# Modulation chunks in two output products and a new schedule for VectorE's share, in a two-block transformer on one core

## The chip, the cores and the metric

One NeuronCore of a Trainium2 chip runs the whole program in one launch. The metric is the device time of one execution in microseconds (us); smaller is better.

## The reference

Two blocks of two layers each work on 256 tokens of width 1024, with 256 context tokens beside them in the first layer of each block. All arithmetic is fp32. What the change touches is the modulation: every layer multiplies the activation of a condition vector with a 1024 x 6144 matrix, once for the tokens and once for the context, and cuts the result into six parts (shift, scale and gate of the mixer, shift, scale and gate of the FFN).

```python
# block 1, one layer
m_lat = [m[:, None, :] for m in jnp.split(jax.nn.silu(c) @ ada_w[l] + ada_b[l], 6, axis=-1)]
h_lat = modulate(x_lat, m_lat[0], m_lat[1])            # x * (1 + scale) + shift
y_lat, y_ctx = even_mixer(...) if l % 2 == 0 else odd_mixer(...)   # both end in y @ w_out
x_lat = layer_norm(DN_ALPHA * x_lat + m_lat[2] * y_lat, ln_g[l, 0], ln_b[l, 0])
f_lat = conv_ffn(modulate(x_lat, m_lat[3], m_lat[4]), ...)          # up, conv of 3, silu(g)*a, down
x_lat = layer_norm(DN_ALPHA * x_lat + m_lat[5] * f_lat, ln_g[l, 1], ln_b[l, 1])
# block 2, one layer: rms_norm in place of layer_norm, a mixer of three gated branches, SwiGLU
h = rms_norm_2(xl, g_pre_mix[l]) * (1.0 + sc1) + sh1
y, yc = token_mixer(h, hc, ...)                                     # ends in m @ w_out
xl = xl + gt1 * rms_norm_2(y, g_post_mix[l])
h = rms_norm_2(xl, g_pre_ffn[l]) * (1.0 + sc2) + sh2
xl = xl + gt2 * rms_norm_2(swiglu(h, w_ffn_in[l], w_ffn_out[l]), g_post_ffn[l])
```

In the first layer of a block the context runs through the same steps (512 tokens in all, "T=512"); in the second only the 256 tokens do ("T=256").

## The kernel before

A product of an fp32 weight is made of three TensorE products: SyncE (SP) loads a weight tile of 512 KB (`wr`, 4 buffers), ScalarE casts it (`wh`, L162), VectorE subtracts (`wl`, L164; 3 buffers of each), and TensorE multiplies the high parts and the two mixed pairs (`mm3`; the data's halves are `hH`/`hL`, `gH`/`gL`, `yH`/`yL`). SP issues its loads in program order, and a load waits until its `wr` buffer is free.

The program runs in stages: `even_mixer` (to about 266 us of the span), `b1_out` (the mixer's output product, residual and layer norm, then 128x128 transposes, L370, of the normalised rows `z`), `b1_ffn` with T=512, `odd_mixer`, `b1_out` (T=256), `b1_ffn` (T=256), then block 2: `b2_mixer` and `b2_ffn` with T=512, `b2_mixer` (2070 to 2437 us) and `b2_ffn` with T=256. The even mixer's order is written by a planner that weaves the projection's products with the attention's steps; elsewhere a scheduler orders each engine's instructions by the program's order and its own estimate of when they are ready.

A modulation part (`ada`, `a0` to `a3` for the four layers) is a list of items: eight chunks of 128 x 1024 weights, then a bias and, for most parts, a turn (two transposes, L243). A chunk has two forms. As *quarters* (L198 on `wr`) TensorE multiplies it with the condition at once. On VectorE (`onto`, L205 and L208) each of one or two condition rows is one `adacc` instruction, and at the part's end TensorE sums the result with *pick* products (L198 on `adacc`). A chunk is a load in the `wr` buffers in either form.

Who places the items: the even mixer takes them with `stream_ada` (so many items to each of its six groups, the rest at its end); the T=512 FFNs take them on VectorE with `share_ada`, which adds a number (`SHARE`) to a credit at each call, after an up pair (`up_share`) and after every unit of a down product (`each`), and issues the chunks that the credit pays for; the T=256 FFN of block 1 takes one chunk per up pair (`run_ada`). In a T=512 FFN the order is: up pairs j = 0 to 10, the down product of their outputs in two halves (`nb`) of six units, the evacuation of each half (`tm`, L1098, and `x`, L1101), up pairs 11 to 21, and the second down product. `idle_work` holds the layer norm's affine steps, put off into the up pairs.

## Time and profile before

| | |
|---|---|
| median of 3 runs | 2647.53 us (2646.34 to 2651.3) |
| the profiled execution | 2645.67 us, span 2643.9 us |
| TensorE busy | 2506.0 us (95%) |
| VectorE busy | 1914.5 us (72%) |
| ScalarE busy | 1226.1 us (46%) |
| mean granted TensorE clock | 0.982 |
| loads on SP's queue | 386.45 MB, 47.0% of the 16 DMA engines' span |
| chain that ended last | TensorE 68%, VectorE 15%, issue 5%, ScalarE 5%, DMA 4% |

Busy shares are means over stages with different limits. The granted clock is a share of 2.4 GHz; a stretch at 0.5 runs at 1.2 GHz.

### The profile page before, as it was taken

What the parts mean: (1) busy time and instruction counts of PE and PEld (TensorE: products, weight loads), DVE (VectorE), ACT (ScalarE), POOL (GpSimd) and SP (SyncE); (2) the same over time, 40 slices, a digit from 0 to 9 for tenths busy, and PEclk for the clock granted to TensorE, in tenths of its full rate; (3) what the DMA queues carried; (4) which work ended last, traced back from release to release, by engine and by line L of the source; (5) the groups of instructions that cost most, each with busy time, mean ns of one, the idle gap of its engine ahead of it and who ended that gap; (6) DMA issues with size and microseconds to landing.
All of it is one profiled execution on the core that took longest, in us unless ns stands there. A gap on an engine that the chain in (4) does not pass through costs nothing.

```text
span 2643.9 us, 40529 instructions
## 1 busy us (share of the span) xinstructions
PE 2506.0 (95%) x15364; PEld 2181.9 (83%) x15364; DVE 1914.5 (72%) x3347; ACT 1226.1 (46%) x2329; POOL 323.2 (12%) x411
## 2 busy tenths in 40 slices
PE   7998999899998899999989999999999999898998
PEld 5887797688876898899877878887887999798997
DVE  5866887776878977557779855767666788886554
ACT  3655463134455555556652233632224556554543
POOL 5321100000131000242320000001000100000000
PEclk9999999999999899999989999999999999999999
DMA  8344664664656676531212334556774522356564
GB/s 272 102 127 153 225 184 132 192 205 138 189 172 209 206 234 199 172 91 54 61 50 88 88 100 147 176 177 210 245 234 144 156 80 62 102 155 211 170 181 147
DMA packets 129827, 412.36 MB, mean 156 GB/s; under 512 B 16640, under 2 KB 24992, under 8 KB 129632
## 3 DMA queue, kind: packets, MB, share of 16 engines
q1 hardware_dynamic: 119296, 386.45, 47.0%
q0 software_dynamic: 10048, 23.30, 2.8%
q8 instruction: 121, 1.98, 0.3%
q14 instruction: 74, 0.61, 0.1%
q10 hardware_dynamic: 288, 0.02, 0.0%
HBM read 408.59 MB, written 1.11 MB: 155 GB/s over the span
## 4 chain that ended last, share of the span: by engine, by line
PE 68%; DVE 15%; issue 5%; ACT 5%; DMA 4%; POOL 2%; SPq 0%; DVEq 0%; POOLq 0%; ACTq 0%
PE mm L171 62%; DVE wl L164 3%; PE ax L171 3%; POOL rs_r L310 1%; DMA wr<-in_ada_w 1%; ACT wh L162 1%; DMA s0w<-in_ada_w 1%; PE ax L629 1%; PE ax L618 1%; DVE ptl L633 1%; DVE adacc L208 1%; PE mm L198 1%; DMA wr<-in_w_mod 1%; ACT p L1526 1%; DVE cv L1669 1%
## 5 line engine op out<-in xcount | busy, mean ns | idle before, releaser
L162 ACT CAST wh<-wr 128x1024 fp32r<-128x1024 f32 (+2 forms) x580 | 572.6, 990 | 855.0 <-PE mm L171 591.2
L164 DVE TENSOR_TENSOR wl<-wr,wh 128x1024 fp32r<-128x1024 f32 (+2 forms) x518 | 600.9, 1162 | 287.9 <-ACT wh L162 285.1
L171 PE MATMUL mm<-hH,wh 128*128 128x256 f32 (+1 forms) x2176 | 711.8, 328 | 5.5 <-ACT wh L162 3.9
L171 PE MATMUL mm<-hH,wl 128*128 128x256 f32 (+1 forms) x2176 | 706.5, 325 | 7.4 <-DVE wl L164 4.9
L171 PE MATMUL mm<-hL,wh 128*128 128x256 f32 (+1 forms) x2176 | 706.6, 325 | 0.7 <-DVE hL L360 0.7
L171 PEld LDWEIGHTS mm<-hH,wh 128*128 128x128 f32 x2176 | 419.4, 193 | 46.2 <-ACT wh L162 6.6
L171 PEld LDWEIGHTS mm<-hH,wl 128*128 128x128 f32 x2176 | 418.4, 192 | 42.2 <-DVE wl L164 10.2
L171 PEld LDWEIGHTS mm<-hL,wh 128*128 128x128 f32 x2176 | 419.0, 193 | 32.1 <-DVE hL L360 1.0
L171 PE MATMUL mm<-wh,hH 128*128 128x384 f32 (+1 forms) x864 | 277.8, 322 | 0.7 <-DVE hH L356 0.7
L171 PE MATMUL mm<-wl,hH 128*128 128x384 f32 (+1 forms) x864 | 268.5, 311 | 1.8 <-DVE wl L164 1.8
L171 PE MATMUL mm<-wh,hL 128*128 128x384 f32 (+1 forms) x864 | 268.6, 311 | 0.3 <-DVE hL L360 0.3
L171 PE MATMUL mm<-wl,gH 128*128 128x512 f32 x528 | 207.7, 393 | 5.7 <-DVE wl L164 5.7
L171 PE MATMUL mm<-wh,gH 128*128 128x512 f32 x528 | 206.8, 393 | 6.2 <-DVE acc L1170 4.7
L171 PE MATMUL mm<-wh,gL 128*128 128x512 f32 x528 | 207.3, 393 | 0.0
L208 DVE SCALAR_TENSOR_TENSOR adacc<-wr,cs,adacc 128x1024 f32<-128x1024 f32 x126 | 159.1, 1282 | 40.1 <-DMA wr<-in_w_mod 26.7
L171 PEld LDWEIGHTS mm<-wh,hH 128*128 128x128 f32 x864 | 163.8, 190 | 7.6 <-issue 4.8
L171 PEld LDWEIGHTS mm<-wl,hH 128*128 128x128 f32 x864 | 163.9, 190 | 4.2 <-DVE wl L164 2.6
L171 PEld LDWEIGHTS mm<-wh,hL 128*128 128x128 f32 x864 | 163.5, 189 | 0.5 <-DVE hL L360 0.5
L1669 DVE SCALAR_TENSOR_TENSOR cv<-u,cconv_w,cv 128x512 f32<-128x512 f32 (+1 forms) x240 | 151.9, 636 | 2.6
L164 POOL TENSOR_TENSOR wl<-wr,wh 128x768 fp32r<-128x768 f32 (+1 forms) x62 | 124.1, 2011 | 180.9 <-ACT wh L162 166.2
L310 POOL TENSOR_TENSOR rs_r<-rs_v,mhalf 128x1 f32<-128x1 f32 x44 | 42.2, 960 | 701.0 <-DVE rs_v L331 392.4
L171 PEld LDWEIGHTS mm<-wh,gH 128*128 128x128 f32 x528 | 99.7, 189 | 29.5 <-issue 7.1
(339 smaller groups left out, 3974.6 us busy)
## 6 DMA issues: line engine op xcount, KB each, us to landing
wr<-in_up SPq DMA_DIRECT2D x192, 512.0 KB, 4.3
wr<-in_dn SPq DMA_DIRECT2D x100, 512.0 KB, 4.0
wr<-in_w_mod SPq DMA_DIRECT2D x96, 512.0 KB, 4.7
wr<-in_ada_w SPq DMA_DIRECT2D x80, 512.0 KB, 4.3
wr<-in_wg SPq DMA_DIRECT2D x48, 512.0 KB, 3.6
wr<-in_glu SPq DMA_DIRECT2D x24, 512.0 KB, 3.8
wr<-in_qkv SPq DMA_DIRECT2D x32, 384.0 KB, 3.1
wr<-in_wo SPq DMA_DIRECT2D x24, 512.0 KB, 4.1
```

The lines of the kernel that those rows point to most:

```text
L162: nc.scalar.copy(h[:, :n], w[:, :n])
L164: eng.tensor_tensor(l[:, :n], w[:, :n], h[:, :n], ALU.subtract)
L171: self.nc.tensor.matmul(o, s, m, start=start, stop=stop, skip_group_check=True)
L198: nc.tensor.matmul(st["pa"][32 * j:32 * j + 32, 0:256], a, x[:, j * 256:(j + 1) * 256], start=start, stop=stop, skip_group_check=True, til ...
L208: nc.vector.scalar_tensor_tensor(st["acc"][r], wt, cs[:, k, r:r + 1], st["acc"][r], ALU.mult, ALU.add)
L310: self.nc.gpsimd.tensor_tensor(o, i, self.mhalf[:, 0:n], ALU.pow)
L618: nc.tensor.transpose(pt[:, i * P:(i + 1) * P], s, self.idr)
L629: nc.tensor.transpose(pt[:, i * P:(i + 1) * P], s, self.idn)
L633: nc.vector.tensor_tensor(L, pt, H, ALU.subtract)
L1526: nc.scalar.activation(p, bs[s], AF.Exp, bias=nm[:, s:s + 1], scale=1.0, accum_out=a)
L1669: nc.vector.scalar_tensor_tensor(o, cb["u"][c][:, :, j:j + 256], cb["w"][:, c, j:j + 1], o, ALU.mult, ALU.add)
```

## The change

The chunks of three modulation parts move, and the rules of VectorE's share change. `a1[1]` goes from VectorE in the first FFN to quarters in the even mixer, with other numbers of items per group. `a2[3]`, the quarters of the T=256 FFN of block 1, and `a3[5]`, on VectorE in the T=512 FFN of block 2, become the `fill` of the output product of the T=256 stages: their eight chunks are loaded by `fill_loads` into tiles (`fl`) of the stage's own pool, ahead of the product, and their quarters stand behind it. In the T=512 FFNs the share is left out after the up pairs 9 to 11 (in block 1 after all up to 11) and after the last unit of a down half, its numbers are larger, and the affine steps start one or two pairs earlier.

```diff
--- before.py
+++ after.py
@@ -84,7 +84,8 @@
 class Builder:
     SKEW = 4
 
-    SHARE = {1: (2.0, 2.6), 2: (3.4, 2.2)}
+
+    SHARE = {1: (2.2, 2.6), 2: (4.0, 2.4)}
 
     def __init__(self, tc, A, out):
         self.tc, self.nc, self.A, self.out = tc, tc.nc, A, out
@@ -274,6 +275,23 @@
         if not items:
             self.credit = 0
 
+    def fill_loads(self, pool, items):
+
+        res = []
+        for ap, f, _ in items:
+            t = None
+            if ap is not None:
+                t = pool.tile([P, D], F32, name=self.nm("fl"))
+                self.nc.sync.dma_start(t, ap)
+            res.append((t, f))
+        return res
+
+    def fill(self, loaded):
+        bank, self.ada_bank = self.ada_bank, "mm"
+        for t, f in loaded:
+            f(t)
+        self.ada_bank = bank
+
     def stream_ada(self, ws, items, n):
 
         res = []
@@ -404,7 +422,7 @@
                 for t in tiles:
                     step(t, u, ws[u])
             if each:
-                each()
+                each(u)
         if tail:
             for t in tiles:
                 for u in (nu - 2, nu - 1):
@@ -930,7 +948,7 @@
         groups, units = [], []
         for g in range(6):
             gr, un = group(g)
-            gr["extra"] = self.stream_ada(ws, ada, (0, 6, 6, 6, 6, 6)[g])
+            gr["extra"] = self.stream_ada(ws, ada, (0, 4, 5, 5, 5, 5)[g])
             groups.append(gr)
             units += un
         last = self.stream_ada(ws, ada, 100)
@@ -1124,7 +1142,7 @@
     def ystat(self, k, t):
         return self.yH[k][:, t * P:(t + 1) * P], self.yL[k][:, t * P:(t + 1) * P]
 
-    def b1_out(self, w, tiles, key, l):
+    def b1_out(self, w, tiles, key, l, fill=()):
 
         with ExitStack() as st:
             pool = self.pool(st, "chain")
@@ -1137,6 +1155,7 @@
             self.cwb = self.vecs(f"conv_w{l}", 44 * 3, self.lnp).rearrange("p (c j) -> p c j", j=3), self.vecs(f"conv_b{l}", 44, self.lnp)
             self.y_split(pool, len(tiles) * P)
             self.new_hT()
+            fill = self.fill_loads(pool, fill)
             late = []
             for s in segs:
                 ts_ = (2 * s, 2 * s + 1)
@@ -1145,6 +1164,7 @@
                     for t in ts_:
                         self.resid1(pool, t, nb, banks[t], gts[s], True)
                 late += self.ln1(s, g_bc, b_bc, ab)
+            self.fill(fill)
 
             self.idle_work = late
 
@@ -1179,7 +1199,7 @@
                     o = self.psum("mm")
                     self.mmF(o[:, :n], w, 0, 8, lambda k: self.rhs(k, c0, c1))
                     bk.append(o)
-                if j >= self.SKEW + 2 and self.idle_work:
+                if j >= self.SKEW + (blk == 1 and T == 512) and self.idle_work:
                     self.idle_work.pop(0)()
                 s = pool.tile([P, 512], F32, tag="sil", name=self.nm("sil"), bufs=2)
                 if blk == 1:
@@ -1207,8 +1227,7 @@
                     res.append((w_dn[kh, nb][:, k0:k1, :].rearrange("p k n -> p (k n)"), [11 * kh + k for k in range(k0, k1)]))
                 return res
             def up_share(j):
-
-                if j < self.SKEW + 2 or not self.idle_work:
+                if j not in (9, 10, 11) and (blk == 2 or j > 11):
                     self.share_ada(ada, self.SHARE[blk][0])
             if T == 512:
                 for s in range(2):
@@ -1219,7 +1238,7 @@
                     up_pair(j, 0, 2)
                     up_share(j)
                 for nb in range(2):
-                    banks = self.mmT(units(0, nb), gstat, range(4), 512, each=lambda: self.share_ada(ada, self.SHARE[blk][1]))
+                    banks = self.mmT(units(0, nb), gstat, range(4), 512, each=lambda u: self.share_ada(ada, self.SHARE[blk][1]) if u < 5 else None)
                     for t in range(4):
                         evac(t, nb, banks[t], 0)
                 for j in range(11, 22):
@@ -1685,7 +1704,7 @@
             cb["pd"].append(pd)
         return [f for gi in range(4) for f in self.mmF_items(ws, self.A[f"wp{l}"][gi], lambda k: self.rhs(k, 0, T), T, done)]
 
-    def b2_mixer(self, l, T, cb, after, ws, pre, rate):
+    def b2_mixer(self, l, T, cb, after, ws, pre, rate, fill=()):
         nc, A = self.nc, self.A
         key = f"b2l{l}"
         nseg = T // 256
@@ -1711,6 +1730,7 @@
                     ys = [pool2.tile([P, D], F32, name=self.nm("ym")) for _ in tiles]
                     self.new_hT()
                     ab = self.AB(gpre, None, self.modT[key][3], self.modT[key][4])
+                    fill = self.fill_loads(pool2, fill)
                     sums = {}
                     for s in range(nseg):
                         ts_ = (2 * s, 2 * s + 1)
@@ -1722,6 +1742,7 @@
                         for t in ts_:
                             self.post2(t, ys[t], sums)
                         self.rms_hT([s], ab, sums)
+                    self.fill(fill)
 
     def b2_branches(self, sm, st, mp, l, T, nseg, yT, m, sy, cb, taps):
 
@@ -1918,7 +1939,7 @@
                 yp = self.pool(s1, "yT")
                 self.yT_tiles(yp, 512)
                 with ExitStack() as s2:
-                    self.even_mixer(self.pool(s2, "att"), a0[2] + a0[4] + a0[3] + a0[5])
+                    self.even_mixer(self.pool(s2, "att"), a0[2] + a0[4] + a0[3] + a0[5] + a1[1])
                 xpool = self.pool(st, "x", side="right")
                 self.x = []
                 for t in range(4):
@@ -1928,7 +1949,7 @@
                 self.ln_open(4)
                 with ExitStack() as s2:
                     self.b1_out(A["ev_out"], [0, 1, 2, 3], "b1l0", 0)
-            self.b1_ffn(0, 512, a1[1] + a1[0] + a1[2] + a1[4] + a1[3], "b1l1")
+            self.b1_ffn(0, 512, a1[0] + a1[2] + a1[4] + a1[3], "b1l1")
             self.lst.close()
             a2 = self.ada("b2l0", 2, A["w_mod"][0], A["b_mod"][0])
             with ExitStack() as s1:
@@ -1941,7 +1962,7 @@
                 cb = [self.conv_pool(sc[0], 0, 512)]
                 self.ln_open()
                 with ExitStack() as s2:
-                    self.b1_out(A["od_out"], [0, 1], "b1l1", 1)
+                    self.b1_out(A["od_out"], [0, 1], "b1l1", 1, a2[3])
             ws = Stream(self, 10)
             ab2 = []
 
@@ -1955,7 +1976,7 @@
                 self.rms_hT([0], ab2[0])
                 for f in self.glu_items(ws, 0, cb[0], 1, 2):
                     f()
-            self.b1_ffn(1, 256, a2[3], None, early, late, a1[5])
+            self.b1_ffn(1, 256, [], None, early, late, a1[5])
             self.lst.close()
 
             def after(l):
@@ -1965,10 +1986,10 @@
                 self.ln_open()
             a3 = self.ada("b2l1", 2, A["w_mod"][1], A["b_mod"][1], ctx=2)
             self.b2_mixer(0, 512, cb[0], lambda: after(0), ws, self.glu_items(ws, 0, cb[0], 0, 1), 1.0)
-            self.b2_ffn(0, 512, a2[5] + a3[1] + a3[0] + a3[2] + a3[4] + a3[3] + a3[5], False)
+            self.b2_ffn(0, 512, a2[5] + a3[1] + a3[0] + a3[2] + a3[4] + a3[3], False)
             self.lst.close()
             ws = Stream(self)
-            self.b2_mixer(1, 256, cb[1], lambda: after(1), ws, self.glu_items(ws, 1, cb[1], 0, 1), 0.6)
+            self.b2_mixer(1, 256, cb[1], lambda: after(1), ws, self.glu_items(ws, 1, cb[1], 0, 1), 0.6, a3[5])
             self.b2_ffn(1, 256, [], True)
             self.lst.close()
```

VectorE in the first FFN (T=512), at the end of the first down product, before. `wl_5399` and `wl_5430` (L164) are the splits of up pair 11; L208 are chunks, L1098 and L1101 the evacuation:

```order
L208 SCALAR_TENSOR_TENSOR adacc_5341<-wr_5378,cs_85,adacc_5341 128x1024
L1098 TENSOR_TENSOR tm_5384<-mm_5149,gbc_1125_5133 128x512
L208 SCALAR_TENSOR_TENSOR adacc_5341<-wr_5381,cs_85,adacc_5341 128x1024
L1101 SCALAR_TENSOR_TENSOR x_3200<-x_3200,tm_5384 128x512
L1098 TENSOR_TENSOR tm_5387<-mm_5150,gbc_1125_5133 128x512
L1098 TENSOR_TENSOR tm_5390<-mm_5151,gbc_1126_5135 128x512
L1101 SCALAR_TENSOR_TENSOR x_3202<-x_3202,tm_5387 128x512
L1101 SCALAR_TENSOR_TENSOR x_3204<-x_3204,tm_5390 128x512
L1098 TENSOR_TENSOR tm_5393<-mm_5152,gbc_1126_5135 128x512
L164 TENSOR_TENSOR wl_5399<-wr_5396,wh_5398 128x1024
L1101 SCALAR_TENSOR_TENSOR x_3206<-x_3206,tm_5393 128x512
L164 TENSOR_TENSOR wl_5430<-wr_5427,wh_5429 128x1024
```

and the same place now, by the changed kernel's lines (L165 is the split, L209 a chunk, L235 a part's bias, L1116 and L1119 the evacuation; `wl_5417` and `wl_5448` are pair 11's):

```order
L165 TENSOR_TENSOR wl_5345<-wr_5342,wh_5344 128x1024
L209 SCALAR_TENSOR_TENSOR adacc_5287<-wr_5372,cs_85,adacc_5287 128x1024
L165 TENSOR_TENSOR wl_5387<-wr_5384,wh_5386 128x512
L165 TENSOR_TENSOR wl_5417<-wr_5414,wh_5416 128x1024
L235 TENSOR_TENSOR adas_5380<-ax_5375,adab_5282 128x256
L165 TENSOR_TENSOR wl_5448<-wr_5445,wh_5447 128x1024
L1116 TENSOR_TENSOR tm_5402<-mm_5167,gbc_1126_5151 128x512
L1116 TENSOR_TENSOR tm_5405<-mm_5168,gbc_1126_5151 128x512
L1119 SCALAR_TENSOR_TENSOR x_3256<-x_3256,tm_5402 128x512
L1119 SCALAR_TENSOR_TENSOR x_3258<-x_3258,tm_5405 128x512
L1116 TENSOR_TENSOR tm_5408<-mm_5169,gbc_1127_5153 128x512
L1116 TENSOR_TENSOR tm_5411<-mm_5170,gbc_1127_5153 128x512
```

The chunks of that part now stand ahead of the last two splits of the down half, and the splits of pair 11 ahead of the evacuation instead of behind it.

SP's queue at the output product of the first block's T=256 stage now (`od_out` is its weight in eight loads, of which the fourth stands first here, `fl` the early chunks; before, the eight loads followed one another):

```order
L155 DMA wr_8745<-in_od_out 128x1024
L285 DMA fl_8673<-in_w_mod 128x1024
L285 DMA fl_8675<-in_w_mod 128x1024
L285 DMA fl_8677<-in_w_mod 128x1024
L285 DMA fl_8679<-in_w_mod 128x1024
L285 DMA fl_8681<-in_w_mod 128x1024
L285 DMA fl_8683<-in_w_mod 128x1024
L285 DMA fl_8685<-in_w_mod 128x1024
L285 DMA fl_8687<-in_w_mod 128x1024
L155 DMA wr_8771<-in_od_out 128x1024
L155 DMA wr_8789<-in_od_out 128x1024
L155 DMA wr_8807<-in_od_out 128x1024
```

The second half of the weight stands behind eight chunks of 512 KB.

TensorE behind that product, before:

```order
L171 MATMUL mm_8748<-wl_8794,yH_8634 128x512
L171 MATMUL mm_8748<-wh_8793,yL_8642 128x512
L370 MATMUL ax_8849<-idn,z_8836 128x128 x2
L370 MATMUL ax_8850<-idn,z_8836 128x128 x2
L370 MATMUL ax_8851<-idn,z_8836 128x128 x2
L370 MATMUL ax_8852<-idn,z_8836 128x128 x2
L370 MATMUL ax_8849<-idn,z_8847 128x128 x2
L370 MATMUL ax_8850<-idn,z_8847 128x128 x2
L370 MATMUL ax_8851<-idn,z_8847 128x128 x2
L370 MATMUL ax_8852<-idn,z_8847 128x128 x2
L171 MATMUL mm_8908<-hH_8659,wh_8904 128x256
```

and now (L199 are quarters, L388 the transposes):

```order
L172 MATMUL mm_8770<-wl_8816,yH_8640 128x512
L172 MATMUL mm_8770<-wh_8815,yL_8648 128x512
L199 MATMUL mm_8916<-fl_8673,cs_90 32x256 x4
L199 MATMUL mm_8916<-fl_8675,cs_90 32x256 x4
L199 MATMUL mm_8916<-fl_8677,cs_90 32x256 x4
L199 MATMUL mm_8916<-fl_8679,cs_90 32x256 x4
L199 MATMUL mm_8916<-fl_8681,cs_90 32x256
L388 MATMUL ax_8871<-idn,z_8858 128x128 x2
L388 MATMUL ax_8872<-idn,z_8858 128x128 x2
L388 MATMUL ax_8873<-idn,z_8858 128x128 x2
L388 MATMUL ax_8874<-idn,z_8858 128x128 x2
L199 MATMUL mm_8916<-fl_8681,cs_90 32x256 x3
```

Four chunks and a quarter of the fifth stand between the product and the first transposes, the rest behind those. In block 2 all of them stand ahead of the transposes.

## Rows read from the trace of the kernel before

**Rows 1.** The page: busy time by engine.

```profile
PE 2506.0 (95%) x15364; PEld 2181.9 (83%) x15364; DVE 1914.5 (72%) x3347; ACT 1226.1 (46%) x2329; POOL 323.2 (12%) x411
```

**Rows 2.** Stretches: us; busy us of PE, PEld, DVE, ACT, POOL; clock, DMA share, GB/s.

```profile
239.00:267.00 28.00, 19.26 (x140) 12.81 (x132) 19.96 (x39) 14.73 (x32) 3.16 (x6) 0.92 0.61 193
...
444.00:460.00 16.00, 11.29 (x42) 8.59 (x41) 11.72 (x14) 4.14 (x6) 0.00 (x0) 0.89 0.50 148
...
487.00:496.00 9.00, 5.80 (x20) 4.36 (x19) 9.00 (x8) 1.06 (x1) 0.00 (x0) 0.81 0.63 191
...
515.00:531.00 16.00, 11.05 (x38) 7.88 (x37) 12.96 (x18) 3.14 (x3) 0.00 (x0) 0.79 0.80 262
...
843.00:857.00 14.00, 11.84 (x44) 9.38 (x45) 9.54 (x16) 7.93 (x14) 5.77 (x18) 0.88 0.93 320
...
869.00:889.00 20.00, 10.59 (x56) 9.61 (x56) 18.65 (x28) 7.57 (x17) 6.22 (x6) 0.66 0.58 188
...
888.00:1088.00 200.00, 200.00 (x1452) 184.81 (x1451) 151.39 (x235) 113.23 (x169) 7.23 (x14) 1.00 0.68 213
...
2380.00:2404.00 24.00, 23.12 (x192) 22.71 (x191) 17.99 (x32) 10.12 (x15) 0.00 (x0) 1.00 0.73 231
...
2436.00:2452.00 16.00, 9.29 (x46) 8.10 (x45) 11.75 (x20) 8.55 (x20) 2.78 (x6) 0.68 0.47 143
```

**Rows 3.** TensorE timeline, first FFN: start, us, instruction, [idle before <-releaser].

```profile
448.51 0.47 PE L171 MATMUL mm<-wh,gH 128*128 128x512 f32 x1 [1.94 <-DVE acc L1170]
...
453.12 0.47 PE L171 MATMUL mm<-wh,gH 128*128 128x512 f32 x1 [2.78 <-DVE acc L1170]
...
491.68 0.80 PE L171 MATMUL mm<-wl,gH 128*128 128x512 f32 x1 [3.20 <-DVE wl L164]
...
521.26 0.50 PE L171 MATMUL mm<-hH,wh 128*128 128x512 f32 x1 [2.71 <-ACT wh L162]
...
525.46 0.80 PE L171 MATMUL mm<-hH,wl 128*128 128x512 f32 x1 [1.73 <-DVE wl L164]
```

**Rows 4.** VectorE timeline in the same places.

```profile
485.61 4.88 DVE L208 SCALAR_TENSOR_TENSOR adacc<-wr,cs,adacc 128x1024 f32<-128x1024 f32 x4
...
510.51 5.24 DVE L208 SCALAR_TENSOR_TENSOR adacc<-wr,cs,adacc 128x1024 f32<-128x1024 f32 x4
```

**Rows 5.** TensorE timeline: a chunk between products; two parts' picks.

```profile
942.61 0.28 PE L171 MATMUL mm<-hH,wl 128*128 128x256 f32 x1
...
942.82 0.64 PE L198 MATMUL ax<-wr,cs 128*32 128x256 f32 x8
...
943.61 0.28 PE L171 MATMUL mm<-hL,wh 128*128 128x256 f32 x1
...
508.80 1.07 PE L198 MATMUL ax<-adacc,pick 128*32 128x256 f32 x16
```

**Rows 6.** SP timeline: chunk loads of the odd mixer; the second half of od_out.

```profile
817.27 16.88 SPq L154 DMA_DIRECT2D wr<-in_w_mod  x11
...
843.82 8.94 SPq L154 DMA_DIRECT2D wr<-in_od_out  x4
```

**Rows 7.** DMA, 843 to 861 us: GB/s in 40 slices; issues, median us to landing.

```profile
GB/s 100 246 309 291 159 214 164 182 218 264 255 319 391 378 432 360 395 346 319 401 374 382 364 420 393 399 380 392 386 370 346 331 423 191 137 118 155 328 382 228
...
wr<-in_od_out SPq DMA_DIRECT2D x4, 512.0 KB, 7.6
```

**Rows 8.** Timelines: od_out starts; a cast, a split; a change, transposes in block 2.

```profile
844.81 0.47 PE L171 MATMUL mm<-wh,yH 128*128 128x512 f32 x1 [2.00 <-ACT yH L816]
...
852.82 1.05 ACT L162 CAST wh<-wr 128x1024 fp32r<-128x1024 f32 x1 [1.68 <-PE mm L171]
...
871.95 1.22 DVE L164 TENSOR_TENSOR wl<-wr,wh 128x1024 fp32r<-128x1024 f32 x1
...
1811.17 0.50 PE L171 MATMUL mm<-wh,gH 128*128 128x512 f32 x1 [1.49 <-DVE sil L1192]
...
2442.34 1.94 PE L370 MATMUL ax<-idn,z 128*128 128x128 f32 x8 [5.73 <-ACT z L1314]
```

## Prediction

> **What bounds the kernel now.** I read the page first: TensorE is busy 2506 of 2643.9 us and VectorE 1914.5 [rows 1], so the kernel ends sooner only if TensorE does fewer products, waits less, or runs its products at the higher of its two clock levels. The stretches come next [rows 2], because the 95% is a mean. From 888 to 1088 us TensorE is busy 200.00 of 200 us at a granted clock of 1.00: whatever leaves TensorE there is a gain of the same size. Around the changes of product in the first FFN, and behind the two output products of the T=256 stages, it is different: 10.59 busy of 20 us from 869, and 9.29 of 16 from 2436, at a mean clock of 0.66 and 0.68. Third, TensorE's timeline says what those stretches wait for. In the first FFN the gaps are 1.94 and 2.78 us at the first change (for `acc`, VectorE's convolution), 3.20 at the second (for a `wl`), and 2.71 and 1.73 at the third (for a `wh`, then for a `wl`) [rows 3]. VectorE's own timeline, fourth, shows what stands ahead there: four `adacc` for 4.88 us from 485.61 and four for 5.24 us from 510.51 [rows 4]. Those are the share. Last, the DMA views say whether a load can be brought forward: the stretch 843 to 857 us has a DMA share of 0.93 already [rows 2].
>
> **The change part by part**, against the profiled execution's 2645.7 us. The median of the runs shown is 2647.5, so 1.9 us are added at the end.
>
> *The changes of product in the first FFN.* The second and third change lose 3.20 + 2.71 + 1.73 = 7.6 us in gaps [rows 3]. With them goes time at 1.2 GHz: a mean clock of 0.81 over 9 us is 0.19 x 2 x 9 = 3.4 us at half, and 0.79 over 16 us is 6.7 us [rows 2]. Products at half speed lose half of their time, so at most 5.0 us more. The order shows that here the change does what it says: pair 11's splits stand ahead of the evacuation, no longer behind eight `adacc` and most of the evacuation. At the first change it is less clear: the scheduler pulls the chunks of the down product's share forward, and as many `adacc` as before, sixteen, still stand among the last convolutions. It loses 4.7 us in gaps and at most 0.11 x 16 = 1.8 us of clock. I take 10 of 12.6 for the last two and 2 of 6.5 for the first: **-12**, bounds 0 and -19.
>
> *Chunks that leave TensorE in the second FFN.* Between the product that starts at 942.61 and the second one behind it, at 943.61, stands one chunk; without it two starts of 0.12 us each would lie there [rows 5], so a chunk costs 1.00 - 0.24 = 0.76 us. Eight make 6.1, and two turns some 0.4: **-6.5**, bounds -5, with eight of the 0.64 that its own row shows, and -6.5, as the stretch has no idle time to swallow it [rows 2].
>
> *Picks.* Sixteen take 1.07 us [rows 5]; `a1[1]` loses sixteen and `a3[5]` eight. With the restarts of the products about them, **-1.9**.
>
> *Eight more chunks in the even mixer.* By 0.76 they are 6.1 us of TensorE. The planner now puts 19 chunks where before 7 stood, from 238 us on. TensorE is busy there 19.26 of 28 us [rows 2], so 8.7 us of idle time can take some of the twelve. Two thirds hidden: **+2**. Bounds: -2, if the fuller stretch keeps the clock that falls at its end, 0.92 in the mean [rows 2], and +20, if each of the twelve waits for its load. The nearest pace is the odd mixer's, where eleven loads went out in 16.88 us [rows 6]: (16.88 - 0.37) / 10 = 1.65 us each. SP's output weight stands behind all of them.
>
> *The fill of `od_out`.* The quarters cost little: 9.4 of the 20 us from 869 are idle [rows 2], about those transposes, and eight chunks in a row take some 4 us of that (sixteen such products, the size of two chunks, take 1.07 us in a row [rows 5]). The loads cost more. On SP they stand ahead of the second half of the weight, and the first of them waits for the last attention product, because its tile takes that stage's memory. 8 x 0.524 MB at about 370 GB/s, the plateau of the slices [rows 7], are 11.3 us. The fifth load went out at 843.82 [rows 6] and took about 7.6 us [rows 7], so it was there at 851.4; with a cast and a split, 1.05 + 1.22 us [rows 8], it was ready at 853.7, and needed when the product, which starts at 844.81 [rows 8] and is 24 us long, is half done, at 857. That slack of 3.3 us stands against 11.3 of delay: TensorE waits **+8** in mid-product. Bounds: 0, if the weight gets through beside the chunks, and +14, with 6.7 us at the lower clock behind the wait as at the third change [rows 2]. Late next are the loads of the FFN behind it, by as much.
>
> *The second FFN at T=512 (block 2).* Eight `adacc` of some 1.25 us [rows 4] go, and there is no share at its changes. The longest gap is 1.49 us, behind pair 10 [rows 8], with two like it further on: **-2**, bounds 0 and -4.
>
> *The fill in block 2.* The quarters stand in 5.73 us of idle time [rows 8] and hide. The eight loads stand among the weights of the merge, where the DMA share is 0.73 for 24 us [rows 2], which leaves 0.27 x 24 = 6.5 us for 11.3 us of loads. The rest is late for a product whose weights come in steps, with some buffers of slack: **+3**, bounds 0 and +8.
>
> The sum is -12 - 6.5 - 1.9 + 2 + 8 - 2 + 3 = **-9.4 us**: 2636.3 for a profiled execution, 2638 us for the median. A measurement of this kernel can tell 0.2%, 5.3 us, from no change.
>
> The rule that would speak for these early loads is in the Trainium skill, "DMA: Bandwidth & Descriptors", section "Rules for kernel authors": issue a DMA early, compute, and wait late. The same page, under "Issuing engines are not separate DMA queues", speaks against them, since all loads share the same 16 engines; the share of 0.93 agrees with that. By the first alone the sum would be -20.4, by the second it stays.
>
> **The rivals.**
>
> *The loads are hidden.* If the fill's loads find room in both places, +8 and +3 become 0: -20.4, or 2627 us. For it: after 857 us the slices fall to 118 to 233 GB/s in places. Against it: the share of 0.93 before that, and the order on SP. It could be more, as 0.34 x 2 x 20 = 13.6 us at half clock stand from 869 and 0.32 x 2 x 16 = 10.2 from 2436 [rows 2]; if TensorE, now at work in these gaps, kept the higher clock, some 5 and 4 us of products would come back. The Trainium skill, "TensorE: Matmul & The Clock Gate", section "Part 1: The HAM clock gate", puts it so: activity releases the throttle. In this trace the clock fell behind each gap of over 2.7 us read above, which agrees. I give the case 0.17.
>
> *The share moves, the gaps stay.* The same number of `adacc` runs in the same FFN less 16, and a split that waits at unit 4 of a half is as bad as one at its end. Then -12 becomes -2, and the sum +0.6: 2648 us. For it speaks the first change, whose order hardly differs. Chance 0.12.
>
> *The even mixer becomes bound by its loads* (slower). 12 chunks at 1.65 us make +19.8 in place of +2, and the sum +8.4: 2656 us. It decides from (14.7 + 2) / 12 = 1.4 us of added time per chunk on, where the total passes +5.3. For it: four buffers only, and TensorE's order is fixed, so that each chunk that waits for a load holds up the attention step behind it. Against it: four are loaded ahead, and the stretch has 8.7 us idle. Chance 0.13.
>
> *The change does not do what it says* (the scheduler places the work where it was): 2647.5 us. The orders exclude most of it; 0.03.
>
> **How the numbers follow.** The forecast, a sum between -17 and -2, has 0.55; with the hidden loads 0.17, the gaps that stay 0.12, the even mixer 0.13, nothing 0.03. Of the forecast's 0.55, 0.45 lies over 5.3 us faster and 0.10 within; the hidden loads are all faster; of the gaps that stay 0.01 is faster, 0.09 the same, 0.02 slower; of the even mixer 0.02 the same, 0.11 slower. Together: faster 0.63, same 0.24, slower 0.13. The range reaches from 2624, past the hidden loads with little of the clock, to 2654, short of the even mixer's full price; the forecast's own is 2630 to 2646.
>
> **What would show it.** Right: no gap over 1 us at the second and third change of the first FFN; 200 us of the second FFN shorter by 6 us; a gap of 5 to 9 us in the middle of the T=256 `od_out` product, for a `wl` or `wh` of its fifth load; quarters in the idle time behind it. Wrong: gaps for loads of `in_ada_w` between attention steps from 240 us on, a first output product that starts well after 267 us, or gaps in the first FFN that have moved to another unit. If `od_out` runs through without a gap, the largest positive term falls.

## The result, and the profile after

The changed kernel is slower: 2664.14 us, the median of 4 runs (2662.87 to 2665.84), against 2647.86 of the kernel before, a ratio of 1.006 with the 95% interval 1.0043 to 1.0077. The prediction, 2638 us within 2624 to 2654 and faster with 0.63, was wrong in sign and in range. The span of the profiled execution went from 2643.9 to 2661.7 us. The page of the profile after, busy time by engine and the chain that ended last:

```profile
PE 2512.1 (94%) x15468; PEld 2184.3 (82%) x15468; DVE 1892.9 (71%) x3323; ACT 1225.6 (46%) x2329; POOL 322.3 (12%) x411
...
PE 69%; DVE 15%; DMA 5%; ACT 5%; issue 3%; POOL 2%; SPq 0%; DVEq 0%; POOLq 0%; ACTq 0%
```

TensorE has 6.1 us more of busy time than in [rows 1] and 17.8 us more of span, so some 12 us are new waiting. The page does not say where. The starts of the same TensorE instructions in both traces do. The table gives for each stretch how much longer (+) or shorter (-) it is than before, in us, in the changed kernel and in all experiments (named below). It is read from one profiled execution of each kernel, whose time lies up to 5.5 us from that kernel's median (e1: 2649.59 against 2655.12; e12: 2629.14 against 2634.04). "Attention" is the first of the `pth` products, L172, with which the last four attention steps of the even mixer begin.

| stretch ends at | before, us | after | e1 | e11 | e2 | e6 | e5 | e4 | e8 | e7 | e9 | e12 |
|---|---|---|---|---|---|---|---|---|---|---|---|---|
| even mixer: last attention | 242.49 | +11.1 | +1.0 | +8.5 | +12.2 | +5.2 | +10.8 | +9.6 | +1.0 | -0.4 | +0.8 | +9.8 |
| first output product | 267.22 | +15.4 | +0.1 | +1.8 | -0.1 | +14.6 | +15.4 | +13.1 | +0.8 | +0.5 | +1.7 | +0.6 |
| first FFN: down | 443.69 | +0.7 | -0.1 | +0.2 | -0.1 | +2.3 | +1.0 | +2.5 | +0.1 | +0.1 | -0.6 | -0.9 |
| pair 11 | 521.26 | -14.1 | -16.1 | -16.1 | -14.3 | -14.0 | -13.9 | -13.9 | -16.1 | -16.1 | -16.1 | -14.3 |
| second down | 648.89 | -5.8 | +10.2 | +10.4 | -5.8 | -5.8 | -5.9 | -5.9 | -3.9 | -3.8 | -3.8 | -5.9 |
| `od_out` product | 844.81 | -0.4 | +2.5 | +5.7 | -0.8 | +0.4 | -1.5 | -0.9 | +1.1 | +0.7 | +1.6 | -0.7 |
| its transposes | 871.49 | +10.5 | +10.4 | +10.0 | +10.7 | +10.0 | -0.6 | +11.1 | -0.6 | -0.5 | -2.6 | -1.3 |
| second FFN: down | 1019.98 | -8.3 | -8.1 | -7.5 | -7.9 | -8.5 | -5.0 | -8.4 | +0.4 | -4.9 | -4.4 | -4.4 |
| block 2, T=512: down | 1805.45 | -2.0 | -0.9 | -0.5 | +1.8 | -1.6 | -0.2 | +3.0 | -0.9 | +0.6 | -1.0 | -1.7 |
| pair 11 | 1869.99 | +3.4 | +1.7 | +2.8 | +0.8 | +3.2 | +3.5 | -1.5 | -1.8 | -1.8 | -3.2 | -2.0 |
| second down | 1993.49 | +3.2 | +0.6 | +0.6 | +4.6 | +3.0 | +4.8 | +0.2 | +0.8 | +1.1 | +0.2 | +0.2 |
| T=256 output product | 2413.96 | +2.5 | +2.0 | +6.0 | +3.2 | +2.6 | +3.1 | +1.9 | +0.5 | +0.4 | +3.8 | +3.3 |
| end of the last product | 2635.61 | +1.6 | +0.6 | +0.9 | +1.0 | +0.7 | +0.9 | +1.1 | +0.0 | +0.2 | +0.5 | +0.6 |

Where two kernels have the same code in a stretch, their entries differ by 1 to 4 us (+11.1, +10.8 and +9.6 in the first row; +2.5 and +6.0 in the last but one), so a single entry below that says nothing. Five stretches carry the result: the even mixer costs 26.5 us, `od_out` 10.5 and block 2's FFN 6.6, the first FFN gives 19.9 and the second, behind `od_out`, 8.3.

The first FFN did what was hoped. Stretches of after, around its three changes of product (columns as in [rows 2]):

```profile
464.00:480.00 16.00, 15.76 (x71) 12.73 (x70) 14.91 (x17) 6.81 (x9) 0.00 (x0) 1.00 0.59 184
500.00:520.00 20.00, 20.00 (x101) 15.76 (x100) 14.22 (x19) 2.10 (x2) 1.99 (x4) 1.00 0.54 177
530.00:550.00 20.00, 20.00 (x95) 15.97 (x94) 17.05 (x21) 6.19 (x7) 3.16 (x6) 1.00 0.74 242
```

TensorE was busy 11.29 of 16, 5.80 of 9 and 11.05 of 16 us there at clocks of 0.79 to 0.89 [rows 2]; now it hardly waits, and the clock is 1.00. The losses are elsewhere. TensorE's timeline of after, the waits in the even mixer, in `od_out` and in block 2:

```profile
77.75 1.81 PE L647 MATMUL ax<-idn,p 128*128 128x128 f32 x8 [2.96 <-DVE p L710]
...
137.85 0.58 PE L172 MATMUL mm<-ptl,v 128*128 128x256 f32 x1 [4.85 <-DVE ptl L651]
...
261.66 1.22 PE L172 MATMUL ax<-bias,idn 128*128 128x256 f32 x2 [4.54 <-DMA bias<-in_nb_bias]
...
272.48 0.72 PE L199 MATMUL mm<-wr,cs 128*32 128x256 f32 x8 [1.91 <-DMA wr<-in_ada_w]
...
284.17 0.64 PE L199 MATMUL mm<-wr,cs 128*32 128x256 f32 x8 [1.76 <-DMA wr<-in_ada_w]
285.68 0.64 PE L199 MATMUL mm<-wr,cs 128*32 128x256 f32 x8 [0.88 <-DMA wr<-in_ada_w]
...
293.72 1.22 PE L172 MATMUL mm<-wh,yH 128*128 128x512 f32 x2 [2.37 <-ACT yH L834]
...
873.32 1.22 PE L172 MATMUL mm<-wh,yH 128*128 128x512 f32 x2 [8.29 <-ACT wh L163]
...
1820.51 0.79 PE L172 MATMUL mm<-wh,gH 128*128 128x512 f32 x1 [3.67 <-DVE sil L1212]
```

The 2.37 us before the first output product were there before; the other waits are new or longer. The first of them stands at the first attention step, whose transposes of `p` the kernel before reached without a wait:

```profile
74.30 1.29 PE L629 MATMUL ax<-idn,p 128*128 128x128 f32 x8
```

About these waits the clock falls. The stretches of after that hold the end of the even mixer, and the long wait in `od_out` with the products behind it:

```profile
250.00:294.00 44.00, 30.42 (x231) 17.06 (x232) 18.11 (x40) 12.70 (x29) 8.10 (x16) 0.84 0.72 241
...
865.00:889.00 24.00, 15.52 (x84) 11.19 (x84) 13.85 (x19) 7.34 (x7) 1.49 (x1) 0.86 0.74 264
```

In the first, 0.16 x 2 x 44 = 14 us of the stretch were granted 1.2 GHz only, in the second 0.14 x 2 x 24 = 6.7 us.

### The profile page after: what moved, and what is told of

Read it like the earlier page. It is cut to its first block, busy times and chain, and to the rows that moved or that the text cites. A ratio compares the mean times of both kernels' runs of the same rounds, so it can differ in the third digit from the quotient of the medians.

```text
span 2661.7 us, 40708 instructions
## 1 busy us (share of the span) xinstructions
PE 2512.1 (94%) x15468; PEld 2184.3 (82%) x15468; DVE 1892.9 (71%) x3323; ACT 1225.6 (46%) x2329; POOL 322.3 (12%) x411
## 4 chain that ended last, share of the span: by engine, by line
PE 69%; DVE 15%; DMA 5%; ACT 5%; issue 3%; POOL 2%; SPq 0%; DVEq 0%; POOLq 0%; ACTq 0%
PE mm L172 62%; DVE wl L165 3%; PE ax L172 3%; POOL rs_r L328 1%; ACT wh L163 1%; DMA s0w<-in_ada_w 1%; PE ax L636 1%; DMA wr<-in_w_mod 1%; PE mm L199 1%; PE ax L647 1%; DVE ptl L651 1%; DMA gbc<-gd 1%; DMA wr<-in_ada_w 1%; DMA wr<-in_od_out 1%; DVE adacc L209 1%
## 5 line engine op out<-in xcount | busy, mean ns | idle before, releaser
L165 DVE TENSOR_TENSOR wl<-wr,wh 128x1024 fp32r<-128x1024 f32 (+2 forms) x518 | 600.7, 1162 | 288.2 <-ACT wh L163 284.8
L172 PE MATMUL mm<-hH,wh 128*128 128x256 f32 (+1 forms) x2176 | 708.2, 326 | 4.8 <-ACT wh L163 3.5
L172 PE MATMUL mm<-hH,wl 128*128 128x256 f32 (+1 forms) x2176 | 704.4, 324 | 7.1 <-DVE wl L165 7.0
L172 PE MATMUL mm<-hL,wh 128*128 128x256 f32 (+1 forms) x2176 | 704.3, 324 | 0.0
L172 PEld LDWEIGHTS mm<-hH,wh 128*128 128x128 f32 x2176 | 417.5, 192 | 41.4 <-ACT wh L163 5.5
L172 PEld LDWEIGHTS mm<-hH,wl 128*128 128x128 f32 x2176 | 416.9, 192 | 41.2 <-DVE wl L165 9.5
L172 PEld LDWEIGHTS mm<-hL,wh 128*128 128x128 f32 x2176 | 417.2, 192 | 31.1
L172 PE MATMUL mm<-wh,hH 128*128 128x384 f32 (+1 forms) x864 | 278.7, 323 | 0.7 <-DVE hH L374 0.7
L172 PE MATMUL mm<-wl,hH 128*128 128x384 f32 (+1 forms) x864 | 269.6, 312 | 2.4 <-DVE wl L165 2.4
L172 PE MATMUL mm<-wh,hL 128*128 128x384 f32 (+1 forms) x864 | 269.5, 312 | 0.3 <-DVE hL L378 0.3
L172 PE MATMUL mm<-wh,gH 128*128 128x512 f32 x528 | 207.2, 393 | 3.9 <-DVE sil L1212 3.7
L172 PE MATMUL mm<-wl,gH 128*128 128x512 f32 x528 | 207.0, 392 | 3.1 <-DVE wl L165 3.1
L172 PE MATMUL mm<-wh,gL 128*128 128x512 f32 x528 | 206.7, 391 | 0.0
L172 PEld LDWEIGHTS mm<-wh,hH 128*128 128x128 f32 x864 | 164.5, 190 | 7.7 <-issue 4.8
L172 PEld LDWEIGHTS mm<-wl,hH 128*128 128x128 f32 x864 | 164.6, 191 | 5.3 <-DVE wl L165 3.6
L209 DVE SCALAR_TENSOR_TENSOR adacc<-wr,cs,adacc 128x1024 f32<-128x1024 f32 x105 | 132.8, 1281 | 50.3 <-DMA wr<-in_w_mod 36.9
L172 PEld LDWEIGHTS mm<-wh,hL 128*128 128x128 f32 x864 | 164.2, 190 | 0.5 <-DVE hL L378 0.5
L165 POOL TENSOR_TENSOR wl<-wr,wh 128x768 fp32r<-128x768 f32 (+1 forms) x62 | 123.9, 2010 | 157.8 <-ACT wh L163 147.3
L172 PEld LDWEIGHTS mm<-wh,gH 128*128 128x128 f32 x528 | 99.8, 189 | 26.5 <-DVE sil L1212 4.1
```

The costliest lines, as they stand in the source:

```text
L165: eng.tensor_tensor(l[:, :n], w[:, :n], h[:, :n], ALU.subtract)
L172: self.nc.tensor.matmul(o, s, m, start=start, stop=stop, skip_group_check=True)
L209: nc.vector.scalar_tensor_tensor(st["acc"][r], wt, cs[:, k, r:r + 1], st["acc"][r], ALU.mult, ALU.add)
```

## The experiments

The theory after the traces: the even mixer has two losses of different cause, one in its attention steps up to 250 us, where VectorE and POOL get in each other's way, and one at its end, where chunks wait for their loads; the loads of the fill displace `od_out`'s weight; and in block 2 the larger `SHARE` puts chunks ahead of `sil`. The rivals: the eight chunks of `a1[1]` cost the even mixer so much wherever they stand; the quarters, not the loads, cost `od_out` its time; block 2 loses by the fill's part that left. Each kernel is the changed one with the edit shown, unless said otherwise.

**e1: `a1[1]` back in the first FFN, the even mixer's old numbers.**

```diff
-(0, 4, 5, 5, 5, 5)[g]
+(0, 6, 6, 6, 6, 6)[g]
...
-self.even_mixer(..., a0[2] + a0[4] + a0[3] + a0[5] + a1[1])
+self.even_mixer(..., a0[2] + a0[4] + a0[3] + a0[5])
...
-self.b1_ffn(0, 512, a1[0] + a1[2] + a1[4] + a1[3], "b1l1")
+self.b1_ffn(0, 512, a1[1] + a1[0] + a1[2] + a1[4] + a1[3], "b1l1")
```

> The changed kernel with one part undone: a1[1] goes back to VectorE in the first FFN (sixteen adacc and the picks) and the even mixer has its old numbers of items. Theory 1 (the even mixer's new order costs 26.5 us, and the first FFN's gain of 20 comes from the rules of the share): the first output product starts at 267 us again, and the sum is 2664 - 26.5 plus 0 to 10 us for the sixteen adacc and the chunks that the credit no longer pays for: 2638 to 2648. Rival (the first FFN's gain comes from the sixteen adacc taken out): 2664 - 26.5 + 20 = 2657, with gaps of over 2 us at the second and third change of product.

Measured 2655.12 us, ratio 1.0024 (1.0014 to 1.0033). The even mixer is back at +1.1 us, but the first FFN gives only 16.1 and loses 10.2 at its end. TensorE's timeline of e1 there:

```profile
642.67 1.08 PE L199 MATMUL ax<-adacc,pick 128*32 128x256 f32 x8 [12.82 <-DVE adacc L209]
```

The time is near the rival's 2657, but not for its reason: TensorE does not wait at the second and third change (22.00 of 22 us busy from 478 us, 20.00 of 20 from 500). The credit does not pay for all chunks of the FFN any more, since the units and pairs at the changes are left out; those that remain run one behind the other at the end of the list, and TensorE waits 12.82 us for their sum. So the move of `a1[1]` and the rules of the share hang together: the rules alone need either fewer chunks or a larger `SHARE`.

**e11: the same without the old numbers** ((0, 4, 5, 5, 5, 5), and no `a1[1]` in the even mixer).

> The changed kernel with the eight chunks of a1[1] back in the first FFN, but with the changed numbers per group (0,4,5,5,5,5) in the even mixer. If the smaller numbers per group are the cause, that is, the queue of chunks left for the end of the stage (about 11 items here, 7 before, 19 in the changed kernel) waits for loads, the first output product still starts 8 to 15 us later than in the kernel before. If it is the eight chunks as such, wherever they stand, it starts within 2 us of the kernel before, as with (0,6,6,6,6,6). The first FFN is as with a1[1] back and the larger numbers: first half 16 us shorter, 13 us given back at its end, and the whole some 2655 to 2665 us.

Measured 2665.56 us, ratio 1.0059 (1.0044 to 1.0074). The first output product starts 10.3 us later than before, with no more chunks than before, so the numbers are a cause of their own. But the place was named wrongly: 8.5 of the 10.3 us are lost up to the last attention steps, and the queue at the end adds 1.8. TensorE's and VectorE's timelines of e11:

```profile
136.28 0.58 PE L172 MATMUL mm<-ptl,v 128*128 128x256 f32 x1 [4.85 <-DVE ptl L651]
```

```profile
129.27 5.47 DVE L710 TENSOR_SCALAR p<-p,prc 128x256 f32<-128x256 f32 x2
```

It is the wait of the changed kernel, to the hundredth, at the same step. The wait at the first attention step is there too, 2.95 us at 77.75; the first attention product behind it starts 4.0 us later than before. By the trace 24 quarter products (three chunks) fewer than before stand ahead of the last attention steps, so the loss up to there is one of order. That these chunks had covered the waits is a guess; no run shows it.

**e2: larger numbers with all 40 chunks.**

```diff
-(0, 4, 5, 5, 5, 5)[g]
+(0, 8, 8, 8, 8, 8)[g]
```

> The changed kernel with eight items per group in the even mixer instead of four and five, so that the end holds as few chunks as before the change. Theory 1a (the long end costs 16.5 us: 19 chunks at the pace of their loads, and a bias load behind them on POOL): the end is 28 to 30 us long again, the time falls by 14 to 18 us. Theory 1b (what costs is that the eight chunks more are there at all, and that the order of the attention steps against the products changed): the end is shorter but the stretch before it longer by as much, and the time falls by less than 6 us.

Measured 2649.35 us, ratio 1.000 (0.9989 to 1.001). The 15.4 us at the end of the stage are gone: -0.1. From the last attention steps to the output product 40 quarter products (5 chunks) remain, where the changed kernel has 132 and the kernel before 48. The body of the stage stays 12.2 us longer. So the eight chunks cost the stage 12.1 us in this order and 26.5 in the changed one: what they cost depends on where they stand.

**e6: the even mixer's splits all on VectorE.** In both kernels those from the ninth on, sixteen by the trace, stand on POOL.

```diff
-ws = Stream(self, 8, pool, 768)
+ws = Stream(self, None, pool, 768)
```

> The changed kernel with all weight splits of the even mixer on VectorE (in the changed kernel three of them ran on POOL for 5.39 us, and VectorE's normalisation of p took 5.21 us instead of some 0.3 beside them). Theory (VectorE and POOL hold each other up there, which in the new order falls on the attention's path): no normalisation over 1.3 us, the gap of 4.85 us before 138 us goes with 6.8 us at the lower clock behind it, and the even mixer is 5 to 8 us shorter. Rival (the attention step is late for another reason, the moved chunks ahead of it on TensorE): the gap stays at over 3 us. VectorE does more splits, which may cost up to 4 us elsewhere in the stage.

Measured 2658.63 us, ratio 1.0039 (1.0026 to 1.0053), 6.7 us less in the even mixer. VectorE's and POOL's timelines of the changed kernel at 130 us, and then VectorE's of e6:

```profile
130.84 5.47 DVE L710 TENSOR_SCALAR p<-p,prc 128x256 f32<-128x256 f32 x2
```

```profile
130.50 5.39 POOL L165 TENSOR_TENSOR wl<-wr,wh 128x768 fp32r<-128x768 f32 x3
```

```profile
130.84 0.62 DVE L710 TENSOR_SCALAR p<-p,prc 128x256 f32<-128x256 f32 x2
```

The same two instructions at the same time take 5.47 us beside three POOL splits and 0.62 without them. The 4.85 us that TensorE waited at 137.85 hang on them: in e6 it waits 0.85 us for that `ptl`. The wait at the first attention step is not of this kind. It stays at 2.75 us in e6, without any split on POOL. By instruction, the form's shortest, median and longest in after and in e6 (ns), with first and last start:

```profile
L710 DVE TENSOR_SCALAR p<-p,prc x96: 341/481/5209, 77.1 to 845.8; 128x512 f32<-128x512 f32 x64, 128x256 f32<-128x256 f32 x32
```

```profile
L710 DVE TENSOR_SCALAR p<-p,prc x96: 344/480/708, 76.9 to 840.3; 128x512 f32<-128x512 f32 x64, 128x256 f32<-128x256 f32 x32
```

One of 96 took 5.21 us, and with the splits away none took more than 0.71.

**e5: the fill's loads later in `od_out`**, from within the loop: behind the sixth weight tile in SP's order rather than ahead of the last four.

```diff
-            fill = self.fill_loads(pool, fill)
             late = []
...
+                if s == segs[-1]:
+                    fill = self.fill_loads(pool, fill)
```

> The changed kernel with the early chunks' loads of the first fill issued behind the output weight's last loads (two of the eight still ahead of the last two) instead of ahead of its second half. Theory (the gap of 8.29 us in mid-product is the 4.2 MB ahead of the weight): the gap goes, the chunks land by about 875 us before change of origin, beside the transposes, and the time falls by 6 to 9 us. Rival (the sum of the bytes is what counts, and the wait moves to the quarters or to the FFN's first weights): less than 3 us.

Measured 2657.33 us, ratio 1.0028 (1.0016 to 1.0039). SP's queue in the changed kernel, then in e5:

```profile
841.74 7.63 SPq L155 DMA_DIRECT2D wr<-in_od_out  x4
850.27 5.11 SPq L285 DMA_DIRECT2D fl<-in_w_mod  x8
856.61 8.68 SPq L155 DMA_DIRECT2D wr<-in_od_out  x4
```

```profile
841.51 9.86 SPq L155 DMA_DIRECT2D wr<-in_od_out  x6
851.60 1.34 SPq L285 DMA_DIRECT2D fl<-in_w_mod  x2
855.74 2.59 SPq L155 DMA_DIRECT2D wr<-in_od_out  x2
858.38 6.92 SPq L285 DMA_DIRECT2D fl<-in_w_mod  x6
```

Six tiles of the weight now go out in one row, and only two loads of the fill stand ahead of the last two. +10.5 becomes -0.6, with the same quarters behind the product, though ten of them and not 34 stand ahead of the first transposes. The loads cost the time, not the quarters: in the changed kernel, too, 2.81 us lie between the product's last start and the transposes (886.08 to 888.89), against 2.82 before. Part of the cost moves on. Of the 8.3 us that the second FFN gained, 5.0 stay: the `in_up` loads now stand behind the late chunks, their splits hold up the layer norm on VectorE, and TensorE waits 5.38 us for its second `z`, against 3.70 in the changed kernel.

**e4: block 2's old numbers.**

```diff
-2: (4.0, 2.4)
+2: (3.4, 2.2)
```

> The changed kernel with block 2's old numbers of the share (3.4 and 2.2 instead of 4.0 and 2.4), the rules otherwise as changed. If the larger number crowds VectorE ahead of the first change of product in block 2's FFN (a gap of 3.67 us and 6.8 us at the lower clock behind it, against 1.49 and none): the gap is below 2 us and the time falls by 4 to 7 us. Rival (the share after up pairs 5 to 8, where before stood the postponed steps, does it whatever the number): less than 2 us.

Measured 2657.93 us, ratio 1.0029 (1.0018 to 1.0041). Block 2's FFN goes from +6.6 to -1.3 (the rows "pair 11" and "second down"). The table bears it out: the six kernels with (4.0, 2.4) lie between +2.3 and +8.3 in these two rows together, the three with the change's rules and (3.4, 2.2), e4, e9 and e12, between -1.3 and -3.0. So the numbers are the cause, not the part that left. How much they cost is less sure: with the stretch ahead of the two, which holds the up pairs before the first change, the six lie between +1.4 and +8.1, and the three at +1.7, -4.0 and -3.5. VectorE's timeline of the changed kernel at the change that waits 3.67 us, then of e4 at the same change, and TensorE's of e4:

```profile
1810.94 2.48 DVE L209 SCALAR_TENSOR_TENSOR adacc<-wr,cs,adacc 128x1024 f32<-128x1024 f32 x2 [1.30 <-DMA wr<-in_w_mod]
...
1817.38 2.48 DVE L209 SCALAR_TENSOR_TENSOR adacc<-wr,cs,adacc 128x1024 f32<-128x1024 f32 x2 [2.82 <-DMA wr<-in_w_mod]
1819.77 0.68 DVE L1212 TENSOR_TENSOR sil<-sil,mm 128x512 f32<-128x512 f32 x1
```

```profile
1818.20 2.48 DVE L209 SCALAR_TENSOR_TENSOR adacc<-wr,cs,adacc 128x1024 f32<-128x1024 f32 x2 [2.81 <-DMA wr<-in_w_mod]
1820.60 0.68 DVE L1212 TENSOR_TENSOR sil<-sil,mm 128x512 f32<-128x512 f32 x1
```

```profile
1821.34 0.50 PE L172 MATMUL mm<-wh,gH 128*128 128x512 f32 x1 [1.38 <-DVE sil L1212]
```

In both VectorE waits 2.8 us for a chunk's load with `sil` behind it, and TensorE waits for `sil`. But in the changed kernel `sil` starts 7.17 us after the down product (1812.60), in e4 4.88 us after it (1815.72), and TensorE waits 1.38 us for it, about the 1.49 of [rows 8].

**e8, e7, e9: without the moved part.** From e1 on, the question was whether `a1[1]` has to leave the first FFN. e8 is the kernel before with the change's rules for block 1 alone and `SHARE` 3.2 after the up pairs, so that all chunks are paid for; e7 adds the fill of `od_out` with late loads; e9 adds to e7 the change's rules of block 2, with its old numbers, and the fill there. Of their edits against the changed kernel, the line that all three share:

```diff
-SHARE = {1: (2.2, 2.6), 2: (4.0, 2.4)}
+SHARE = {1: (3.2, 2.6), 2: (3.4, 2.2)}
```

> The kernel before with the new rules of the share in block 1's first FFN alone (number 3.2, no fill, no move). It measures the first FFN's term by itself: 12 to 16 us faster than before if the rules do it, 0 to 5 if the gain needed the sixteen adacc taken out as well.

> A combination: the even mixer and block 2 as before the change, the new rules of the share in block 1's first FFN with the larger number 3.2 (so that the credit pays for all chunks by pair 21), and the first fill with its loads behind the output weight. From the stages measured so far: -16 at the first half of the FFN, 0 to +3 at its second half, -0.6 at the output product, -5 in the next FFN: 15 to 21 us faster than before, a ratio of 0.992 to 0.994. Rival (3.2 crowds VectorE in the pairs 12 to 21): a gap of over 2 us there and less than 12 us gained.

> The combination with block 2 as changed too (a3[5] as fill of its output product, the new rules of the share there, with the old numbers 3.4 and 2.2). It measures block 2's part against the combination: by the stages of the run with the old numbers it costs 2 to 4 us (the merge is late by 1.5 to 3, nothing comes back behind it); rival (its loads and quarters are hidden and the second FFN gains 2): 1 to 3 us faster than the combination.

| | us | ratio to before, 95% interval |
|---|---|---|
| e8 | 2627.4 | 0.992 (0.9907 to 0.9932) |
| e7 | 2625.4 | 0.9918 (0.9905 to 0.9932) |
| e9 | 2624.78 | 0.9911 (0.9898 to 0.9925) |

All three beat both kernels by far more than the interval. e8's 20.3 us and e7's 22.3 are more than was expected (12 to 16 and 15 to 21), and e9 came out as neither branch of its expectation has it. Nearly all of it is e8's: in the table the first FFN gives 16.1 + 3.9 = 20.0 us with `a1[1]` still in it, as much as the changed kernel gained there by sending it away. What e7 and e9 add lies within the intervals.

**e12: all four repairs at once, `a1[1]` still in the even mixer** (e2, e4, e5 and e6 together).

> The changed kernel with four repairs at once: (0,8,8,8,8,8) in the even mixer, all of that stage's splits on VectorE, the early chunks of od_out loaded behind its weight's third quarter, and block 2's numbers back at (3.4, 2.2). If the terms add, the even mixer ends 12.1 - 6.7 = 5 us later than before, the first FFN keeps its 20 us, od_out costs nothing and block 2's FFN gains 1 to 3: 18 to 22 us under the kernel before, 2626 to 2630 us, the same as the versions that leave a1[1] in the first FFN within 4 us. If the two causes in the even mixer are one (the late chunks wait because the stage was held up early, or the longer queue on VectorE takes the place of the collision), the first output product starts 10 us or more later than before, and the time is 2633 us or more.

Measured 2634.04 us, ratio 0.9943 (0.9927 to 0.996). It is faster than both kernels, but the terms do not add: the even mixer ends 10.4 us later, not 5, because e2's order had less collision left to remove (its longest TENSOR_SCALAR of this line took 2.07 us; the body of the stage goes from +12.2 to +9.8). Of the 9.8 us, 3.7 are there at the first attention product (77.61 us before, 81.27 in e12), behind one chunk more and this wait on TensorE's timeline of e12:

```profile
77.58 1.29 PE L647 MATMUL ax<-idn,p 128*128 128x128 f32 x8 [1.65 <-DVE p L710]
```

From there to the last attention steps stand eight chunks more, and the other 6.1 us are their price, eight of 0.76 us [rows 5], in a stretch without room. That of the kernel before, between the first and the last attention steps:

```profile
77.00:242.49 165.49, 158.84 (x1137) 140.61 (x1137) 116.07 (x285) 92.20 (x258) 43.13 (x41) 1.00 0.39 120
```

TensorE idles 6.65 of 165.49 us. Why `p` is late at the first attention step no run shows.

## Why the prediction was wrong

The terms against the stretches, in us:

| term | forecast | measured |
|---|---|---|
| even mixer | +2 (-2 to +20) | +26.5 |
| first FFN, with picks | -13.3 | -19.9 |
| `od_out`'s fill | +8 (0 to +14) | +10.5 |
| second FFN | -6.5 | -8.3 |
| block 2's FFN, with picks | -2.6 | +6.6 |
| block 2's fill | +3 (0 to +8) | +2.5 |
| the rest | 0 | -0.1 |

(The picks' 1.9 are put two thirds to the first FFN, sixteen, and one third to block 2's, eight.)

*The even mixer* is the step that failed: "Two thirds hidden", +2 us, for twelve chunks in 8.7 us of idle time. It measured +26.5, in two pieces.

The end, +15.4, was foreseen as a rival. It was given 0.13 and priced at 1.65 us a chunk. Measured are 132 products against 48 there, 10.5 chunks, for 15.4 us: 1.47 each, just above the 1.4 from which the rival decides. That was the nearest row, and the forecast took a third of what the eight added chunks cost TensorE, because of the idle time. The end's stretch, before and after:

```profile
242.49:267.22 24.73, 17.12 (x125) 11.19 (x124) 17.23 (x36) 14.19 (x31) 3.33 (x7) 0.91 0.62 199
```

```profile
253.57:293.72 40.15, 27.19 (x210) 14.93 (x206) 15.37 (x36) 11.48 (x27) 7.82 (x16) 0.83 0.74 250
```

TensorE is busy 10.1 us longer: 6.7 us would be 10.5 chunks of 0.64 [rows 5], and the clock is lower. The chunks did hide in part: the waits for `pth` and `ptl`, 4.5 us before, are down to 0.2. But idle time grew by 5.3 us all the same, for the waits that the forecast put at nothing: 4.90 us for `in_ada_w` (1.91, 1.76, 0.88 and a smaller one), and 4.54 that no one had looked for. POOL's queue in the changed kernel:

```profile
255.92 1.98 POOL L216 DMA_DIRECT2D adab<-in_ada_b  x4 [29.74 <-DVE adas L235]
257.89 0.57 POOL L988 DMA_DIRECT2D bias<-in_nb_bias  x1
```

The bias loads of the next modulation part wait until the part before has used the one buffer (`adas`, L235), and the attention's own bias stands behind them in POOL's order. The prediction counted SP's queue, not POOL's. Whether a second buffer alone would end this wait was not tried; with e2's order it is gone.

The other piece, +11.1 us up to the last attention steps, was in no rival. It is not the price of chunks: by the trace two chunks fewer than before stand ahead of those steps. At the first attention product 4.4 us are lost already, behind the 2.96 us of waiting for `p`; the collision with POOL's splits costs some 6 us by e6. e11 shows that 8.5 us come without a single chunk more, by the numbers per group alone. The forecast costed the chunks that are added and not the ones that are moved.

*The first FFN* was right in mechanism, and too small. The gaps read, 12.4 us [rows 3], and the clock behind them, 5.0 and 1.8 us at most, make 19.2, and with the picks nearly all of it came back. The mis-sized step is the first change, 2 of 6.5, where the order "hardly differs": about as many `adacc` stand there, yet TensorE's wait is below 0.3 us. VectorE's last convolution there, before and after:

```profile
452.23 0.74 DVE L1170 SCALAR_TENSOR_TENSOR acc<-mm,conv_w,acc 128x510 f32<-128x510 f32 x1
```

```profile
475.36 0.74 DVE L1190 SCALAR_TENSOR_TENSOR acc<-mm,conv_w,acc 128x510 f32<-128x510 f32 x1
```

It ends 9.3 us after the down product's start before (443.69), and 5.2 us after it now (470.87). VectorE comes to the change less late, which a count of the `adacc` about it does not show. Which of the new rules does it was not tried.

*The second FFN* had the chunks' price right. The 1.8 us beyond its bound of -6.5 are the clock, as the rival of the hidden loads had it: products of 0.41 us run for 6.4 us behind its first one before (880.80), and for 2.6 us now (898.21).

*`od_out`* was right: a wait of 8.29 us for a `wh` in mid-product, forecast +8; the rest of the 10.5 is products at half speed behind it, which the forecast had in its bound. Early loads on a queue that the weight shares cost 10.5 us there, the same loads issued later none, and 3.3 us in the stage behind (e5). The rule of the Trainium skill, "DMA: Bandwidth & Descriptors", section "Rules for kernel authors", to issue a DMA early and wait for it late, was met by the chunks; what they cost fell on the loads behind them.

*Block 2's FFN* had the wrong sign. "Eight `adacc` go, and there is no share at its changes" did not count that the larger `SHARE` puts more of the other chunks into the pairs before, and that chunks whose loads are late hold up `sil` behind them on VectorE. A bound above nothing was missing: 0 was taken as the worst. Of the second half's +3.2, TensorE's waits of 1.44 and 0.53 us for a `wh` and a `wl` at 1949.68 are a part; e1, with the same numbers, has no wait there, and why is open.

*The rivals.* Hidden loads: excluded by `od_out`. Gaps that stay: excluded by the three stretches. The even mixer bound by its loads: right in sign, and its waits for `in_ada_w` are there. That its price per chunk came so near is in part luck, as only 4.90 of the 15.4 us are such waits. Its 2656 us lacked the other piece, od_out's 2.5 and block 2's 9. Of the prediction's own signs, those of being right in the first FFN and in `od_out` came, and of those of being wrong the waits for `in_ada_w` and the late first output product, at 293.72.

## What to carry to other kernels

Before work is moved into a stage that is ordered by hand, look at what the moved rule does to the work that is already there: a sparser order can cost more than the extra work. A freed slot on an engine counts as room only if the load, every queue the work passes (POOL's too) and the buffers are ready in it. When a rule leaves slots out, raise the rate elsewhere before sending work away: here `SHARE` 3.2 gave the same 20 us without the move.

## What the runs showed of the hardware

A VectorE TENSOR_SCALAR of 128 x 256, 0.35 us long at the same place in e6, took 5.21 us while POOL ran three splits back to back for 5.39 us, and ended 0.16 us behind them (130.84 + 5.21 = 136.05 against 130.50 + 5.39 = 135.89). Two more of the changed kernel began beside the last of three splits, at 179.87 and 211.65; they took 1.58 us each and ended 0.15 us behind it. With the splits on VectorE none was held. The Trainium skill, "SBUF — State Buffer", section "Who interferes with whom", states that a `tensor_scalar` in a two-port mode and a GpSimd instruction exclude each other, and that the later one is blocked for the whole of the other. The trace agrees on the blocking; the mode it does not show. It goes further: VectorE was held not for one POOL instruction but for all three.
